# Cosine-similarity attention: the last pair in two pieces, six V buffers, and another order on every engine

## The chip, the cores and the metric

The kernel runs on one core of a Trainium2 chip. The metric is the device time of one launch in microseconds (us), lower is better.

## The reference

Q, K and V have the shape [8, 12, 512, 64] in float32 and tau is 0.1. For each of the 96 heads:

```python
Q_norm = Q / (np.linalg.norm(Q, axis=-1, keepdims=True) + 1e-10)
K_norm = K / (np.linalg.norm(K, axis=-1, keepdims=True) + 1e-10)
scores = np.einsum('bhqd,bhkd->bhqk', Q_norm, K_norm) / tau
weights = np.exp(scores - np.max(scores, axis=-1, keepdims=True))
weights = weights / (np.sum(weights, axis=-1, keepdims=True) + 1e-10)
return np.einsum('bhqk,bhkd->bhqd', weights, V).astype(np.float32)
```

A score is at most 1/tau = 10, so the kernel takes the exponential without the maximum.

## The kernel before

Two heads make a pair; there are 48 pairs, s = 0 to 47. A list of about 1800 operations, each named by a tuple, is built pair by pair. Which engine does an operation, and what it needs first, stands in the list; the order on each engine is written out by hand in `ORDER`, one row of operation numbers for SP, GpSimd ("pool"), VectorE ("dve"), TensorE ("pe") and ScalarE ("act"). Every engine works through its row in order and waits on semaphores where an operation's needs come from another engine.

The operations of pair s (w is 0 for Q, 1 for K; c counts the four chunks of 128 keys):

- `LD(s,w)` (L299, L296 for pair 0) and `LV(s)` (L302): loads of Q, K and V, 256 KB each, issued by SP. Q and K have 18 buffers, V has ten (`R_V`, the second number of `RINGS`): `LV(s)` needs `VC(s-10)`. `ST(s)` (L503) stores the pair's output; it stands in the same SP row, 12 places of pairs later, and waits for `NRM(s)`.
- `SQ(s,..)`: squares in bf16. From pair 4 on one GpSimd instruction over 1024 columns (L325); pairs 0 to 3 are cut by hand (`SQ_ON`, L319 on GpSimd, L317 on ScalarE). Pair 3 has one GpSimd instruction for Q and one for K.
- `SSQ(s,w)` (L342, TensorE) and `RED(s,w)` (L349 or L353, VectorE): sums of squares of each row.
- `LOG(g)` (L367) and `NEW(g,7)` (L370) on ScalarE for the groups g = 0 to 3 of one pair each: the inverse root as exp(-0.5 ln x). Later groups hold two or four pairs and take Newton steps `NEW(g,k)` on VectorE (L377 to L386).
- `SCL(s,w)` (L404; L246 for pair 0): the rows times the inverse root, in bf16, on VectorE or GpSimd. `TR(s,w)` (L410; L254, L256 for pair 0): four transposes on TensorE. `EVA(s)` (L417; L267 for pair 0): the copy from PSUM to SBUF on VectorE.
- `SCO(s,c)` (L446): the scores of chunk c for both heads, into one of two PSUM slots of two banks each. `EXP(s,c)` (L469): one exponential over 128 x 1024 on ScalarE. `SCO(s,c)` needs the exponential two chunks earlier. For pair 0 and c < 2 both are cut by head: `SCO(0,c,h)`, `EXP(0,c,h)`.
- `VC(s)` (L474): V in bf16 beside a column of ones, on GpSimd. `PV(s,h,i)` (L486): weights times V, with the row sums in column 64. `RCP(s,h)` (L497) and `NRM(s,h)` (L499): reciprocal of the sums and the scaled output on VectorE; `NRM(s)` needs `ST(s-8)`.

The last pair (function `last`) is cut into the entries of `PIECES` = (head, first, end) in blocks of 128 query rows: head 0 whole, head 1 in two halves. Its last exponential `EXP(47,3,k)` (L460), the products `PV(47,k,c)` (L514, one chunk c at a time), `RCP(47,k)` (L525), `NRM(47,k)` (L527) and the store `ST(47,k)` (L531) are made once per piece. Piece 2 accumulates in a spare bank. The store of piece 1 is issued by ScalarE, the others by SP:

```python
P.add(("ST", s, k), "act" if k == 1 else "sp", "ldh" if hi - lo == NT else "ldq", T0 + 100 if k == 1 else s + STORE_AT + k, [("NRM", s, k)],
```

At the start TensorE runs eight warm-up matmuls (L185) and between its first operations fills (L188, negative entries in `ORDER`: so many columns), whose results nobody reads.

Of the kernel before, what the change touches and what calls it, by code (L numbers as in the profile page):

```python
# [106 lines left out]
def bass_cosine_similarity_attention_kernel(  # L107
# [54 lines left out]
    group, first = [], []  # L162
# [122 lines left out]
    def pair(s):  # L285
# [6 lines left out]
        for w, x in ((0, Q), (1, K)):  # L292
            if s == 0:
                for h in range(2):
                    P.add(("LD", 0, w, h), "act" if w else "sp", "ldh", -1000 + h,  [],
                          lambda e, w=w, x=x, h=h: e.dma_start(out=qk[iq][:, w, h], in_=src(x, s)[:, h]), slot=f"head{w}_{h}")  # L296
                continue
            P.add(("LD", s, w), "sp", "ld1" if s == 1 else "ld", s, [*([("SCL", 0, w, 0), ("SCL", 0, w, 1), ("SQ", 0, w, 0), ("SQ", 0, w, 1)] if s == R_QK else [key("SCL", s - R_QK, w), *(squares(s - R_QK, w) if s >= R_QK else [])])],
                  lambda e, w=w, x=x: e.dma_start(out=qk[iq][:, w], in_=src(x, s)),  # L299
                  slot=f"first{s}_{w}" if s <= 3 else f"qk{iq}")  # L300
# [126 lines left out]
    def exps(s, c):  # L427
        if s < 0:
            return []
        if s == NP - 1 and c == NT - 1:  # L430
            return [("EXP", s, c, k) for k in range(3)]
# [109 lines left out]
PIECES = ((0, 0, 4), (1, 0, 2), (1, 2, 4))  # L541
GROUPS = [1, 1, 1, 1, 2, 2, 2, 2, 2, 2, 2, 2, 4]
SQ_ON = {1: ("act", ("act", "pool")), 2: ("act", "pool"), 3: ("pool", "pool")}
# [8 lines left out]
RINGS = 18, 10, 6, 3, 3, 3, 8, 3  # L552
# [17 lines left out]
def slack(s, most):  # L570
# [5 lines left out]
        "7 8 64 65 103 104 11 141 142 66 179 180 105 222 223 143 256 257 181 298 299 224 332 333 258 375 376 300 409 "  # L576
        "410 334 451 452 63 377 102 411 140 453 178 221 485 486 527 528 561 562 487 604 605 529 638 639 255 563 680 681 "
        "297 606 714 715 331 640 756 757 374 682 790 791 408 716 833 834 450 758 867 868 484 792 901 902 526 835 935 "
        "936 560 869 978 979 603 903 1012 1013 637 937 1046 1047 679 980 1080 1081 713 1014 1122 1123 755 1048 1156 "
        "1157 789 1082 1190 1191 832 1124 1224 1225 866 1158 1267 1268 900 1192 1301 1302 934 1226 1335 1336 977 1269 "  # L580
        "1369 1370 1011 1303 1412 1413 1045 1337 1446 1447 1079 1371 1480 1481 1121 1414 1514 1515 1155 1448 1556 1557 "
        "1189 1482 1590 1591 1223 1516 1624 1625 1266 1558 1658 1659 1300 1592 1700 1701 1334 1626 1734 1735 1368 1660 "
        "1768 1769 1411 1702 1445 1736 1479 1770 1513 1555 1589 1623 1657 1699 1733 1767 1797 1811 "
    ),
    "pool": (
        "2 0 1 4 14 27 22 35 69 107 50 144 145 89 182 225 127 165 259 208 301 231 335 378 273 284 307 242 454 412 437 "
        "350 395 471 361 318 488 530 426 460 564 607 641 502 536 683 513 717 579 547 759 590 793 836 655 689 870 624 "
        "666 904 742 731 765 700 938 981 808 819 776 876 1015 1049 910 1083 853 887 921 1125 1066 953 1159 987 964 1021 "
        "1108 998 1032 1193 1227 1270 1304 1097 1131 1210 1165 1338 1142 1372 1253 1321 1176 1199 1287 1415 1242 1310 "
        "1449 1483 1517 1344 1559 1432 1355 1466 1398 1500 1387 1421 1593 1455 1627 1576 1610 1661 1703 1737 1531 1565 "  # L590
        "1686 1644 1542 1599 1720 1771 1633 1754 1790 1675 1709 1743 1777 "
    ),
    "dve": (
        "5 13 15 26 28 19 24 21 32 37 71 73 34 109 78 111 76 80 116 114 147 149 118 152 154 183 156 185 226 228 55 186 "
        "56 187 188 61 189 62 190 94 191 95 193 192 194 195 197 100 262 101 199 260 302 304 229 263 138 264 139 265 233 "
        "266 132 267 133 268 338 269 270 176 271 170 379 171 305 275 177 213 336 214 219 381 220 339 340 309 341 342 "
        "455 343 253 344 345 346 348 247 415 248 413 347 352 382 254 289 457 384 416 290 417 386 295 418 296 419 489 "
        "420 323 421 491 423 324 329 422 330 424 458 428 531 366 533 367 492 372 493 565 494 373 495 462 496 608 497 "
        "400 567 401 499 498 406 500 407 642 504 534 610 442 568 443 569 448 570 449 571 684 572 538 573 476 575 574 "
        "644 577 477 611 718 581 482 576 483 613 686 518 645 519 646 760 647 615 648 524 649 525 650 552 720 652 651 "  # L600
        "553 653 837 794 558 657 796 559 595 762 687 721 596 722 871 723 691 724 601 725 839 726 602 728 629 873 727 "
        "630 729 635 905 636 733 763 907 671 797 798 672 799 677 800 801 678 802 767 804 803 939 806 705 941 706 840 "
        "711 805 712 810 982 908 842 747 984 748 753 754 844 874 1050 781 1018 782 787 788 878 1016 1084 1052 824 942 "
        "825 943 944 912 945 830 946 831 947 949 948 950 951 858 1086 859 864 865 985 955 1019 1160 898 899 892 1128 "
        "893 1126 989 1055 932 926 1162 927 933 1023 1053 1194 1196 969 1087 970 1088 975 1089 976 1090 1228 1091 1057 "
        "1092 1093 1094 1095 1129 1003 1230 1004 1009 1010 1099 1163 1037 1273 1038 1305 1133 1043 1044 1339 1071 1307 "
        "1072 1197 1271 1077 1078 1167 1373 1341 1113 1231 1114 1232 1233 1234 1119 1235 1120 1236 1238 1237 1201 1239 "
        "1240 1147 1375 1148 1276 1153 1154 1244 1274 1342 1181 1418 1182 1416 1450 1187 1278 1308 1188 1518 1215 1452 "
        "1216 1312 1484 1221 1222 1560 1486 1258 1376 1259 1377 1264 1378 1379 1265 1380 1346 1381 1382 1383 1385 1292 "
        "1520 1293 1384 1298 1299 1419 1389 1453 1326 1562 1332 1327 1333 1423 1489 1594 1360 1596 1361 1628 1366 1367 "  # L610
        "1457 1487 1630 1403 1521 1404 1522 1409 1523 1410 1524 1525 1662 1526 1491 1527 1528 1529 1443 1444 1563 1437 "
        "1664 1438 1738 1533 1477 1597 1478 1471 1706 1472 1631 1567 1704 1505 1740 1506 1601 1511 1772 1512 1774 1547 "
        "1665 1548 1666 1667 1668 1669 1670 1672 1671 1635 1673 1553 1554 1581 1582 1707 1677 1741 1587 1588 1711 1615 "
        "1616 1775 1621 1622 1649 1650 1745 1655 1656 1691 1692 1697 1698 1779 1725 1726 1731 1732 1759 1760 1765 1766 "
        "1802 1803 1795 1796 1809 1810 "
    ),
    "pe": (
        "6 -256 -256 -256 -192 23 20 -256 70 36 -128 42 72 33 38 108 39 43 110 46 79 77 48 146 81 148 117 83 115 51 85 "
        "57 58 52 53 87 59 54 153 119 155 184 121 60 227 123 125 90 91 92 93 157 96 97 98 159 99 128 261 161 196 198 "
        "163 134 135 136 200 137 303 129 202 130 232 204 230 131 172 206 173 174 175 337 234 166 167 168 169 236 272 "  # L620
        "238 274 209 240 210 211 212 380 276 215 216 217 218 278 306 308 280 243 249 244 282 250 251 252 310 245 246 "
        "414 312 349 314 351 285 286 316 287 288 456 353 383 291 355 292 293 385 357 294 319 320 321 359 322 490 325 "
        "387 326 327 328 389 362 363 364 365 391 427 425 393 368 532 369 429 370 459 371 431 461 396 433 397 398 399 "
        "435 566 402 463 403 404 405 465 438 439 440 441 467 501 503 469 609 444 445 505 446 447 535 507 537 472 473 "
        "509 474 475 643 511 478 479 539 480 481 541 578 580 543 514 515 516 545 517 685 582 612 520 521 584 614 522 "
        "523 586 548 549 550 551 588 719 616 554 555 556 557 618 591 795 592 620 654 656 622 593 594 761 658 690 597 "
        "598 660 599 600 688 662 838 625 626 664 627 628 872 692 631 632 694 633 634 667 668 696 730 732 698 669 670 "
        "906 734 673 674 675 676 736 764 766 738 701 702 703 740 704 940 768 707 708 709 770 710 807 772 809 743 744 "
        "774 745 746 749 811 841 983 813 750 751 752 815 843 777 778 817 779 783 780 784 845 1017 785 786 847 877 875 "
        "849 820 821 822 851 823 1051 826 879 911 909 881 827 828 829 883 854 855 856 885 857 1085 860 913 861 862 863 "  # L630
        "915 952 954 917 888 889 890 894 919 891 895 896 897 956 1127 986 958 988 928 929 960 930 922 923 931 962 924 "
        "925 1161 990 1020 1022 992 965 966 967 994 968 1195 971 996 972 973 974 1024 1054 1056 1026 999 1000 1028 1001 "
# [61 lines left out]
```

## Time and profile before

| | |
|---|---|
| runs | 191.13, 191.26, 191.09, 191.59 us; median 191.19 |
| profiled execution | 191.13 us; its span 189.0 us |
| granted TensorE clock | 1.0 |
| landing of a 256 KB load, from its issue | Q 4.3, K 5.4, V 5.2 us |
| landing of the last pair's stores | 128 KB 1.7, 64 KB 1.6 us |
| bytes moved | HBM read 37.75 MB, written 12.58 MB, 266 GB/s over the span |

A row of the profile names line, engine, operation and tile as out<-in; then come the count, the busy time with the mean in ns, and the idle time before it with what ended it. In the timeline a row has start, length, engine, line and operation; neighbours of one kind are merged ("x3"). Neighbouring instructions of one engine overlap in these records, so the pace is read from starts or ends, not from lengths. "q" behind an engine's name is its queue: it waits or issues.

### The profile page before, as it was taken

Reading aid. Unit: us, or ns where it says so; the run is one execution under the profiler, and the core shown is the slowest. Engines: PE = TensorE matmul, PEld = TensorE weight load, DVE = VectorE, ACT = ScalarE, POOL = GpSimd, SP = SyncE. Lnnn points to the kernel's source line nnn. Section 1 sums busy time; section 2 is a strip of 40 time slices with the busy share of each in tenths; the row PEclk is TensorE's granted clock in tenths of the full one; section 3 lists DMA queues with packets and bytes.
Section 4 is the critical chain, followed back from the end, with each engine's and each line's share of the span. In section 5 each row is a group of like instructions: output and inputs, shape, how many; then the busy total and the mean of one; then the engine's idle time right before and its main releaser. Section 6 shows DMA issues by size and latency. Waiting matters only on the chain.

```text
span 189.0 us, 6679 instructions
## 1 busy us (share of the span) xinstructions
PE 176.3 (93%) x2726; PEld 110.1 (58%) x2726; DVE 165.1 (87%) x530; ACT 182.1 (96%) x214; POOL 154.9 (82%) x145
## 2 busy tenths in 40 slices
PE   6998999999999999999999899999999999899992
PEld 2555666666565666566666566665666556555552
DVE  2788999999999999999999989998889987977543
ACT  4799999999999999999999999999999999999992
POOL 5599999999999999999999899999699898260000
PEclk9999999999999999999999999999999999999999
DMA  4999998899999898999899987996999944113133
GB/s 158 357 349 351 349 362 303 268 323 360 379 385 373 269 287 269 318 360 311 256 255 352 365 278 238 312 321 207 308 288 350 295 140 131 59 55 114 56 114 111
DMA packets 52445, 50.75 MB, mean 269 GB/s; under 512 B 3136, under 2 KB 52416, under 8 KB 52416
## 3 DMA queue, kind: packets, MB, share of 16 engines
q1 hardware_dynamic: 51984, 50.02, 82.0%
q8 instruction: 21, 0.34, 0.8%
q10 hardware_dynamic: 432, 0.33, 0.5%
q14 instruction: 8, 0.07, 0.1%
HBM read 37.75 MB, written 12.58 MB: 266 GB/s over the span
## 4 chain that ended last, share of the span: by engine, by line
ACT 94%; DMA 3%; SPq 1%; issue 1%; DVE 1%; PE 0%
ACT et L469 92%; DMA qk<-in_Q_dram 3%; SPq L299 0%; SPq L296 0%; ACT et L460 0%; DVE ob L527 0%; ACT sq L317 0%; ACT ys L367 0%; ACT nps L370 0%; PE ops L514 0%; DVE rd L525 0%
## 5 line engine op out<-in xcount | busy, mean ns | idle before, releaser
L469 ACT ACTIVATE et<-scps 128x1024 bf16<-128x1024 f32 (+1 forms) x193 | 175.8, 1249 | 0.0
L325 POOL TENSOR_TENSOR sq<-qk 128x1024 bf16<-128x1024 f32 x44 | 82.8, 1893 | 2.1 <-DMA qk<-in_K_dram 2.1
L446 PE MATMUL scps<-qt 64*128 64x512 bf16 x384 | 75.6, 386 | 7.5 <-ACT et L469 2.3
L486 PE MATMUL ops<-vb,et 128*128 128x65 bf16 x1504 | 74.5, 194 | 0.0
L486 PEld LDWEIGHTS ops<-vb,et 128*128 128x128 bf16 x1504 | 56.0, 98 | 27.9 <-issue 21.5
L404 POOL TENSOR_TENSOR qn<-qk,rk 128x512 bf16<-128x512 f32 x37 | 38.1, 1042 | 6.3 <-DVE rk L382 6.0
L499 DVE TENSOR_TENSOR ob<-ops,rd 128x256 f32<-128x256 f32 x94 | 39.3, 420 | 0.9
L404 DVE TENSOR_TENSOR qn<-qk,nps 128x512 bf16<-128x512 f32 x57 | 38.0, 678 | 0.5 <-ACT nps L370 0.5
L417 DVE COPY qt<-tps 128x1024 bf16<-128x1024 bf16 x47 | 32.3, 688 | 4.1 <-PE tps L410 3.4
L446 PEld LDWEIGHTS scps<-qt 64*128 64x128 bf16 x384 | 19.5, 93 | 26.3 <-ACT et L469 10.2
L410 PE MATMUL tps<-ident,qn 128*128 128x128 bf16 x376 | 33.0, 221 | 0.1
L474 POOL TENSOR_SCALAR vb<-vf 128x512 bf16<-128x512 f32 x48 | 29.3, 626 | 0.8 <-DMA vf<-in_V_dram 0.8
L353 DVE TENSOR_REDUCE nps<-sq 128x8 f32<-128x512 bf16 x44 | 29.7, 683 | 0.2 <-POOL sq L325 0.2
L410 PEld LDWEIGHTS tps<-ident,qn 128*128 128x128 bf16 x376 | 21.4, 98 | 11.9 <-issue 5.9
L497 DVE RECIPROCAL rd<-ops 128x4 f32<-128x4 f32 x94 | 16.6, 177 | 9.0 <-PE ops L486 5.8
L342 PE MATMUL ops<-sq,ident 128*128 128x64 bf16 x400 | 20.0, 193 | 0.3 <-ACT nps L240 0.3
L342 PEld LDWEIGHTS ops<-sq,ident 128*128 128x128 bf16 x400 | 14.9, 98 | 4.5 <-issue 2.9
L349 DVE TENSOR_REDUCE nps<-ops 128x8 f32<-128x64 f32 x44 | 9.3, 211 | 0.8 <-PE ops L342 0.7
L377 DVE TENSOR_TENSOR nps<-nps,ys 128x32 f32<-128x32 f32 (+1 forms) x30 | 6.2, 208 | 0.2
L378 DVE SCALAR_TENSOR_TENSOR nps<-nps,ys 128x32 f32<-128x32 f32 (+1 forms) x30 | 6.2, 207 | 0.2
L185 PE MATMUL ops<-warm_in,ident 128*128 128x512 bf16 x8 | 3.6, 631 | 1.4 <-POOL ident L175 1.4
L319 POOL TENSOR_TENSOR sq<-qk 128x512 bf16<-128x512 f32 (+1 forms) x4 | 3.7, 934 | 1.5 <-DMA qk<-in_K_dram 1.5
(50 smaller groups left out, 41.2 us busy)
## 6 DMA issues: line engine op xcount, KB each, us to landing
vf<-in_V_dram SPq DMA_DIRECT2D x48, 256.0 KB, 5.2
qk<-in_Q_dram SPq DMA_DIRECT2D x47, 256.0 KB, 4.3
qk<-in_K_dram SPq DMA_DIRECT2D x47, 256.0 KB, 5.4
out_dram<-ob SPq DMA_DIRECT2D x47, 256.0 KB, 3.7
qk<-in_Q_dram SPq DMA_DIRECT2D x2, 128.0 KB, 2.6
qk<-in_K_dram ACTq DMA_DIRECT2D x2, 128.0 KB, 2.8
out_dram<-ob SPq DMA_DIRECT2D x1, 128.0 KB, 1.7
out_dram<-ob ACTq DMA_DIRECT2D x1, 64.0 KB, 1.6
```

The lines of the kernel that those rows point to most:

```text
L325: lambda e: e.tensor_tensor(out=sqf, in0=data, in1=data, op=ALU.mult))
L342: last = e.matmul(out=o_ps[bank][:, 320:384], lhsT=ident[:, :], rhs=sq[iqs][:, 8 * w : 8 * w + 8, 8 * k : 8 * k + 8], start=(k == 0), stop ...
L353: lambda e, w=w, dst=dst: e.tensor_reduce(out=dst, in_=sq[iqs][:, 8 * w : 8 * w + 8, :], axis=AX.X, op=ALU.add))
L404: lambda e, w=w, r=r: e.tensor_tensor(out=qn[iqn][:, w].rearrange("p t h d -> p h t d"), in0=qk[iq][:, w].rearrange("p h (t d) -> p h t d" ...
L410: last = e.transpose(t_ps[:, w, t, :], qn[iqn][:, w, t].rearrange("p h d -> p (h d)"), ident[:, :])
L417: lambda e: e.tensor_copy(out=qt[iqt][:, :, :, :].rearrange("p w t x -> p (w t x)"), in_=t_ps[:, :, :, :].rearrange("p w t x -> p (w t x)")))
L446: last = e.matmul(out=sc_ps[:, 2 * b + h, :], lhsT=qt[iqt][64 * h : 64 * h + 64, 1, c, :], rhs=qt[iqt][64 * h : 64 * h + 64, 0, :, :], sta ...
L469: lambda e, c=c, b=b, hs=hs: e.activation(out=et[iet][:, c, hs[0] : hs[-1] + 1, :], in_=sc_ps[:, 2 * b + hs[0] : 2 * b + hs[-1] + 1, :], f ...
L474: lambda e: e.tensor_scalar(out=vb[:, iq, :, :, 0:DIM].rearrange("p c h d -> p h c d"), in0=vf[iv][:, :, :].rearrange("p h (c d) -> p h c ...
L486: last = e.matmul(out=o_ps[h][:, 65 * t : 65 * t + 65], lhsT=et[iet][:, c, h, 128 * t : 128 * t + 128], rhs=vb[:, iq, c, h, :], start=(c = ...
L497: lambda e, h=h, grid=grid: e.reciprocal(out=rd[io][:, h, :], in_=grid[:, :, DIM]))
L499: lambda e, h=h, grid=grid: e.tensor_tensor(out=ob[io][:, h], in0=grid[:, :, 0:DIM], in1=rd[io][:, h, :].unsqueeze(2).to_broadcast([128, N ...
```

## The change

Four places of the code and the five rows of `ORDER`:

```diff
-                  slot=f"first{s}_{w}" if s <= 3 else f"qk{iq}")
+                  slot=f"first{s}_{w}" if s <= 2 else f"qk{iq}")
...
-            return [("EXP", s, c, k) for k in range(3)]
+            return [("EXP", s, c, k) for k in range(len(PIECES))]
...
-PIECES = ((0, 0, 4), (1, 0, 2), (1, 2, 4))
+PIECES = ((0, 0, 4), (1, 0, 4))
...
-SQ_ON = {1: ("act", ("act", "pool")), 2: ("act", "pool"), 3: ("pool", "pool")}
+SQ_ON = {1: ("act", ("act", "pool")), 2: ("act", "pool")}
...
-RINGS = 18, 10, 6, 3, 3, 3, 8, 3
+RINGS = 18, 6, 6, 3, 3, 3, 8, 3
```

So the last pair has two pieces, one per head; pair 3's squares are one GpSimd instruction over Q and K, and its two loads count on one semaphore (`qk3`) in place of one each; V has six buffers, and `LV(s)` needs `VC(s-6)`. Nine operations fall away (the K half of pair 3's squares, and the third piece's exponential, four products, reciprocal, scaling and store).

The order, with numbers turned into names:

- SP: the same sequence, without the third piece's store at the end.
- ScalarE: the same sequence but for `LOG(1)`, which moves from behind `EXP(0,1,0)` to before it, and `LOG(3)`, which moves from before `EXP(1,1)` to behind it:

```diff
- SQ(2,0) EXP(0,1,0) LOG(1) NEW(1,7) EXP(0,0,0) EXP(0,0,1) EXP(0,1,1) LOG(2) EXP(0,2) NEW(2,7) EXP(0,3) EXP(1,0) LOG(3) EXP(1,1) NEW(3,7) EXP(1,2)
+ SQ(2,0) LOG(1) EXP(0,1,0) NEW(1,7) EXP(0,0,0) EXP(0,0,1) EXP(0,1,1) LOG(2) EXP(0,2) NEW(2,7) EXP(0,3) EXP(1,0) EXP(1,1) LOG(3) NEW(3,7) EXP(1,2)
```

- TensorE: two more fills of 256 columns before the first transposes, one more before `SSQ(1,1)`, which moves ahead of `SCO(0,1,0)`; `PV` of many pairs at other places between the scores. The beginning, and the end from the last scores on:

```diff
- warm 256 256 256 192 TR(0,1,0) TR(0,0,0) 256 SSQ(1,0) TR(0,1,1) 128 SCO(0,1,0) SSQ(1,1) TR(0,0,1) SCO(0,0,0) SSQ(2,0) SCO(0,0,1) SCO(0,1,1) SSQ(2,1) SCO(0,2) TR(1,1) TR(1,0) SCO(0,3) SSQ(3,0) SCO(1,0) SSQ(3,1) TR(2,1) SCO(1,1) TR(2,0)
+ warm 256 256 256 256 256 192 TR(0,1,0) TR(0,0,0) 256 SSQ(1,0) TR(0,1,1) 256 SSQ(1,1) 128 SCO(0,1,0) TR(0,0,1) SCO(0,0,0) SSQ(2,0) SCO(0,0,1) SCO(0,1,1) SSQ(2,1) SCO(0,2) TR(1,1) TR(1,0) SCO(0,3) SCO(1,0) SCO(1,1) SSQ(3,1) SSQ(3,0) TR(2,1) TR(2,0)
...
- SCO(47,3) PV(47,0,0) PV(47,1,0) PV(47,0,1) PV(47,1,1) PV(47,2,0) PV(47,1,2) PV(47,1,3) PV(47,0,2) PV(47,0,3) PV(47,2,1) PV(47,2,2) PV(47,2,3)
+ SCO(47,3) PV(46,0,2) PV(46,0,3) PV(47,1,0) PV(47,1,1) PV(47,1,2) PV(47,1,3) PV(47,0,0) PV(47,0,1) PV(47,0,2) PV(47,0,3)
```

- VectorE: `RED(1,0)`, `RED(1,1)` move ahead of `EVA(0,1,1)`; in some 150 places further on neighbours change places, mostly `RED`, `RCP` and `NRM` around `EVA`. At the end both pieces follow each other, head 1 first.
- GpSimd: the memset of `eps` moves behind the other three; `VC` of most pairs and some of `SQ` and `SCL` stand a few places earlier or later.

ScalarE's row ends with `EXP(47,3,1) EXP(47,3,0) ST(47,1)`, where it ended with `EXP(47,3,1) EXP(47,3,0) EXP(47,3,2) ST(47,1)`.

## The prediction

> **What bounds the kernel now.** I read the page first: shares, then the chain of waits, then the costliest groups.
>
> ```profile
> PE 176.3 (93%) x2726; PEld 110.1 (58%) x2726; DVE 165.1 (87%) x530; ACT 182.1 (96%) x214; POOL 154.9 (82%) x145
> L469 ACT ACTIVATE et<-scps 128x1024 bf16<-128x1024 f32 (+1 forms) x193 | 175.8, 1249 | 0.0
> ```
>
> ScalarE's exponentials (L469) are the chain and had no idle time before them. The mean of 1249 ns is no price, since neighbours overlap; the chain in order of time gives the pace:
>
> ```profile
> 15.06 169.56 ACT et L469 x185
> 184.63 0.78 ACT et L460 x2
> ```
>
> 169.56/185 = 0.917 us per exponential, without a gap. So the time has three parts: a head until about 15 us, a body that cannot get shorter while ScalarE does the same 185 exponentials, and a tail. A change in order can cost in the body and gain only at the two ends. Next I read ScalarE in the head:
>
> ```profile
> 8.36 0.58 ACT L469 ACTIVATE et<-scps 128x512 bf16<-128x512 f32 x1
> 8.84 0.30 ACT L367 ACTIVATE ys<-xs,eps 128x16 f32<-128x16 f32 x1
> 9.17 0.19 ACT L370 ACTIVATE nps<-ys 128x16 f32<-128x16 f32 x1
> 9.29 1.55 ACT L469 ACTIVATE et<-scps 128x512 bf16<-128x512 f32 x3
> 10.72 0.32 ACT L367 ACTIVATE ys<-xs,eps 128x16 f32<-128x16 f32 x1
> 10.92 1.03 ACT L469 ACTIVATE et<-scps 128x1024 bf16<-128x1024 f32 x1
> 11.82 0.21 ACT L370 ACTIVATE nps<-ys 128x16 f32<-128x16 f32 x1
> ```
>
> Every start follows the previous end: already here nothing but ScalarE's own order counts. A logarithm (L367) directly before its power (L370) takes 8.84 to 9.29 = 0.45 us; with an exponential between them the two cost 0.20 (10.72 to 10.92) plus 0.11 (11.82 to the next exponential at 11.93) = 0.31.
>
> **Head, TensorE's order.** The sums of pair 1's key squares, SSQ(1,1), move ahead of the first score, SCO(0,1,0). TensorE before:
>
> ```profile
> 7.52 0.22 PE L188 MATMUL scps<-warm_in,ident 128*128 128x128 bf16 x1
> 7.67 0.39 PE L446 MATMUL scps<-qt 64*128 64x512 bf16 x1
> 7.99 0.41 PE L342 MATMUL ops<-sq,ident 128*128 128x64 bf16 x8
> 8.23 0.39 PE L254 MATMUL tps<-ident,qn 128*128 128x128 bf16 x4
> 8.55 0.39 PE L446 MATMUL scps<-qt 64*128 64x512 bf16 x1
> ```
>
> SSQ(1,1) needs GpSimd's half square, whose row (start 7.16, 0.61 us) ends at 7.77; such sums start 0.05 to 0.09 after their square, so 7.84. From there by the rows' own steps: sums to the fill 0.24 (7.99 to 8.23), fill to score 0.15 (7.52 to 7.67), SCO(0,1,0) at 8.23; score to transposes 0.32, 8.55; to SCO(0,0,0) 0.32, 8.87; SSQ(2,0) 9.19; 0.34 later (8.87 to 9.21 before) SCO(0,0,1) at 9.53, where it stood at 9.21. Its result comes at 9.53 + 0.39 = 9.92, and the second exponential of the run at 9.29, which started at 9.77, starts at about 9.94: **+0.17 us**. The logarithm of group 1, now ahead of the first exponential, waits for its sum (7.84 + 0.41, then 0.23 on VectorE) and starts at about 8.53 in place of 8.84; its power no longer stands next to it, and the 0.14 that this saves is spent waiting for that score, so I count nothing. If the score came in time, it would be a gain of 0.1.
>
> **Head, ScalarE's order.** Group 3's logarithm moves behind EXP(1,1), directly before its power: 0.45 in place of 0.30 (13.73 to 13.93 and 14.84 to 14.94). **+0.15 us**. VectorE's SCL(3) waits for that power (0.48 us idle, then 15.10) and goes later by the same 0.3 as ScalarE, so the leads further on stay.
>
> **Head, the rest, at nothing.** Two more 256-column fills before the first transposes cost at most 2 x 0.21 us (the half-rate fills start 4.83, 5.04, 5.25), and the eps memset moved back gives up to 0.10. The transposes at 5.89 go back by 0.2 at most; the copies they feed end at 7.09, while the next reader on TensorE's path is now at 8.23, so about 0.9 us covers it. Without that cover it would be 0.2. The third new fill stands where TensorE waits for 7.77 anyway. Pair 3's squares as one GpSimd instruction cost 1.89 (the L325 row at 13.15) in place of 2.04 for both: 0.15 earlier on an engine that next waits 0.29 for a load. Sharing one semaphore among pair 3's two loads costs nothing, as that square needs both.
>
> The Trainium skill's "TensorE: Matmul & The Clock Gate" (Part 1, What's actually happening) lets the full rate begin after about 3.4 us of steady work; here 256-column fills still start 0.21 apart at 5.25, 3.8 us after the first matmul at 1.44. By the rule the two extra fills would cost 0.22 us together, by the row 0.43; both are covered.
>
> **Body, six V buffers.** LV(s) now waits for VC(s-6). I set each V load's issue beside the conversion six earlier, GpSimd's places taken from the new order: 16 of 42 come too early, by 0.1 to 4.5 us. The worst:
>
> ```profile
> 63.56 1.50 SPq L302 DMA_DIRECT2D vf<-in_V_dram  x1
> 65.10 0.47 SPq L299 DMA_DIRECT2D qk<-in_Q_dram  x1
> ```
>
> ```profile
> 67.95 1.21 POOL L474 TENSOR_SCALAR vb<-vf 128x512 bf16<-128x512 f32 x2
> ```
>
> LV(21) stands until 68; behind it in SP's queue are pair 24's Q and K loads (65.10 to about 68.5) and the stores. Pair 24's squares start at 74.2 and its scaling at 92.5: the delay goes into that distance. From pair 12 on every load was issued 16 us or more before its scaling (least at pair 12: 34.0 to 50.0), of which landing takes about 5, and stores waiting for L499 already hold SP for 46.4 us in all. I count nothing; the other end is rival 2.
>
> **Body, reordering.** EVA (L417) to the pair's first exponential leaves as little as 0.59 us (pair 16) where ScalarE has no gap. Adding up VectorE's durations ahead of each EVA in both orders: EVA(8) has 0.41 more before it and had 0.90 of lead, leaving 0.49, 0.10 short; EVA(16) has 0.41 more, but VectorE idled 0.33 before it, so 0.08 short. All others keep 0.59. Both losses: **+0.2 us**. From both sides: 0 if the least lead seen isn't the least needed, 1.0 if none of the roughly 0.4 us shifts at the tight pairs (8, 16 and one further) is absorbed. I take 0.2, near the low end, because most pairs keep their lead.
>
> **Tail.** VectorE before:
>
> ```profile
> 185.23 0.17 DVE L525 RECIPROCAL rd<-ops 128x2 f32<-128x2 f32 x1 [0.71 <-PE ops L514]
> 185.44 0.29 DVE L527 TENSOR_TENSOR ob<-ops,rd 128x128 f32<-128x128 f32 x1
> 185.78 0.18 DVE L525 RECIPROCAL rd<-ops 128x4 f32<-128x4 f32 x1
> 186.00 0.42 DVE L527 TENSOR_TENSOR ob<-ops,rd 128x256 f32<-128x256 f32 x1
> 186.53 0.29 DVE L527 TENSOR_TENSOR ob<-tps,rd 128x128 f32<-128x128 f32 x1
> ```
>
> Three pieces end at 186.82. After: the last whole exponential ends at 184.62 (two from 182.45, 2.17 us); two of 512 columns at 0.49 each (three took 1.55 in the head) end at 185.11 and 185.60 (before 185.67). Head 1: product 185.16 to 185.47 (0.31 in the chain), reciprocal to 185.67, scaling 185.71 to 186.13. Head 0: product ends 185.96, but VectorE is free only at 186.05; reciprocal to 186.23, scaling 186.27 to 186.69. That is 0.13 earlier. Its store is 128 KB in place of 64: 1.7 us to landing against 1.6. **-0.03 us**. That ScalarE issues the second head's store is no news: before, too, it issues piece 1; nothing is queued behind it there, and its issue (0.35) is over before SP's. SP loses one issue (0.42), the last. Bounds: -0.4 (all of the third piece's 0.40 behind 186.42) and +0.1.
>
> The Trainium skill's "DMA: Bandwidth & Descriptors" (Anatomy of one DMA) speaks against joining pieces at the end: a fixed part and then bytes/436e9, so 64 KB more would be 0.15 us as an estimate. The rows say 0.1; the tail would be +0.02 by the rule.
>
> **Sum.** The profiled execution took 191.13 us (span 189.0). 191.13 + 0.17 + 0.15 + 0.2 - 0.03 = 191.62; the median of the runs is 0.06 above that execution: **191.7 us, +0.27%**. About 0.2% (0.38 us) is what a measurement here can tell from no change.
>
> **Rivals.**
> 1. The body keeps its pace and only the head slips: 191.19 + 0.29 = 191.5, within 0.2%. For it: no gap in 185 exponentials before, and the same work. Against: the tight leads of pairs 8 and 16.
> 2. SP's queue becomes the bound: the V waits push loads so late that GpSimd stands still and the scalings behind it come late. Delays of 3.4 to 4.5 us at LV(21), LV(32) and LV(34), less what the distances cover; if 1 us of it reaches ScalarE, 191.7 + 1.0 = 192.7. For it: 16 waits, and GpSimd's five waits for K loads (2.1 us) show that it can be starved. Against: some 10 us between landing and scaling.
> 3. Faster: the third piece was dear. If the score lands in time (head +0.0), the logarithm gains 0.1 and the tail all of 0.4, 191.19 - 0.5 = 190.7. It decides if head 1's product ends 0.1 us or more earlier than I have it, so that VectorE is free when head 0's arrives. Against: the two scalings of 0.42 in a row.
>
> **Chances.** Forecast 0.48 (191.4 to 192.0; a quarter of it within 0.2%), rival 1 0.22, rival 2 0.18, rival 3 0.12. Slower by over 0.2%: 0.36 + 0.02 + 0.18 = 0.56; within: 0.12 + 0.18 + 0.03 = 0.33; faster: 0.02 + 0.09 = 0.11. Range 191.0 to 192.6: leaves out rival 3 and the upper half of rival 2.
>
> **What would show it.** SCO(0,0,1) at 9.5 and the second 512 exponential after 9.29 at about 9.94; L370 directly behind L367 at about 15.2; the first of the long run of exponentials 0.3 late; SP's waits for L474 up from 3.3 to over 15 us; idle time before L469 near 8 and 16 pairs in; last L527 near 187.2 with the whole shift in. It is wrong if the long run starts no later than 15.1, or if ScalarE's gaps add to over 0.5 us.

## The result, and the profile after

Over 53 runs of the changed kernel and 79 of the kernel before, the medians are 191.7 and 191.2 us: **ratio 1.0024, 95% interval 1.0015 to 1.0034**. The change costs about 0.45 us. The medians are of all runs; the ratios leave out the few executions that were over 1.5% slower than the fastest of their kernel. The profiled execution of the changed kernel took 192.02 us (span 189.9).

The costliest group on the page of the changed kernel:

```profile
L469 ACT ACTIVATE et<-scps 128x1024 bf16<-128x1024 f32 (+1 forms) x193 | 175.8, 1234 | 0.0
```

The same 193 exponentials, the same 175.8 us, and again no idle time before them. This says that the body did not change and the loss lies at the ends. The chain of waits of the changed kernel in order of time (start, duration, what), from the landing of pair 1's K load on:

```profile
2.16 5.43 DMA qk<-in_K_dram
7.59 0.07 issue
7.66 0.62 POOL sq L319
8.28 0.14 issue
8.42 0.39 PE ops L342 x8
8.81 0.06 PE scps L188
8.87 0.32 PE scps L446
9.18 0.33 PE tps L254 x4
9.51 0.32 PE scps L446
9.83 0.34 PE ops L342 x8
10.17 0.33 PE scps L446
10.51 0.02 issue
10.53 1.09 ACT et L469 x2
...
15.58 0.20 ACT ys L367
15.77 0.02 issue
15.80 0.19 ACT nps L370
15.99 169.59 ACT et L469 x185
```

The same view of the kernel before, for its first exponentials:

```profile
2.67 5.14 DMA qk<-in_Q_dram
7.80 0.02 issue
7.83 0.63 ACT sq L317
8.46 0.48 ACT et L469
8.94 0.20 ACT ys L367
9.14 0.02 issue
9.17 0.19 ACT nps L370
9.36 1.49 ACT et L469 x3
```

The reader is to see three things. Before, the first exponentials hung on the landing of pair 2's Q load (7.80) and then on ScalarE's own row: its square of that load (L317), EXP(0,1,0), group 1's logarithm and power, EXP(0,0,0), and EXP(0,0,1), which started at 9.77. The head now hangs on pair 1's key square (L319), then on its sums (L342), and only then come pair 0's scores (L446): that is the new TensorE order. Group 3's logarithm and power (L367, L370) stand next to each other and both lie on the chain. And the body is 169.59 us for 185 exponentials, against 169.56 before.

The head starts from loads, and these do not land at the same time in every execution. So I read each profile by stages between fixed events (times of single instructions and landings in the trace, us; each difference is one subtraction):

| stage | before | after | change |
|---|---|---|---|
| pair 1's K load landed | 7.09 | 7.59 | +0.50 |
| from there to the start of EXP(0,0,1) | 2.68 | 2.94 | +0.26 |
| end of EXP(1,0) to end of EXP(1,2) | 2.13 | 2.27 | +0.14 |
| pair 2's Q load landed to end of EXP(1,2) (the whole head behind the loads) | 8.21 | 8.62 | +0.41 |
| end of EXP(1,2) to end of the last whole exponential (body) | 168.62 | 168.66 | +0.04 |
| from there to VectorE's last instruction | 2.19 | 2.07 | -0.12 |
| from there to the end of the span | 2.21 | 2.28 | +0.07 |

The row of 2.68 and 2.94 is the distance from a fixed event, not one path: before, that exponential waited for pair 2's Q load, 0.71 us behind pair 1's K load, and not for pair 1's.

0.51 (pair 2's Q load landed at 7.80 before and at 8.31 after) + 0.41 + 0.04 - 0.12 + 0.07 = 0.91, and the spans differ by 189.93 - 189.03 = 0.90. The later landing is half of what separates the two profiles, and 0.40 is left for the kernel itself, close to the 0.45 of the medians. Whether the landing belongs to the change is the first question for the experiments.

### The profile page after: what moved, and what is told of

Its sections match the earlier page's. It is cut to its first block, busy times and chain, and to the rows that moved or that the text cites. A ratio compares the mean times of both kernels' runs of the same rounds, so it can differ in the third digit from the quotient of the medians.

```text
span 189.9 us, 6675 instructions
## 1 busy us (share of the span) xinstructions
PE 176.6 (93%) x2729; PEld 110.2 (58%) x2729; DVE 164.9 (87%) x528; ACT 182.3 (96%) x213; POOL 154.9 (82%) x144
## 4 chain that ended last, share of the span: by engine, by line
ACT 92%; DMA 3%; PE 1%; issue 1%; SPq 1%; DVE 1%; POOL 0%
ACT et L469 91%; DMA qk<-in_K_dram 3%; PE scps L446 1%; DVE ob L527 0%; SPq L296 0%; PE ops L342 0%; POOL sq L319 0%; ACT et L460 0%; SPq L299 0%; ACT ys L367 0%; ACT nps L370 0%; PE tps L254 0%; PE ops L514 0%; DVE rd L525 0%; PE scps L188 0%
## 5 line engine op out<-in xcount | busy, mean ns | idle before, releaser
L469 ACT ACTIVATE et<-scps 128x1024 bf16<-128x1024 f32 (+1 forms) x193 | 175.8, 1234 | 0.0
L325 POOL TENSOR_TENSOR sq<-qk 128x1024 bf16<-128x1024 f32 x45 | 84.6, 1893 | 2.4 <-DMA qk<-in_K_dram 1.4
L446 PE MATMUL scps<-qt 64*128 64x512 bf16 x384 | 75.6, 386 | 7.7 <-ACT et L469 2.1
L486 PE MATMUL ops<-vb,et 128*128 128x65 bf16 x1504 | 75.7, 194 | 0.0
L446 PEld LDWEIGHTS scps<-qt 64*128 64x128 bf16 x384 | 19.4, 93 | 27.2 <-ACT et L469 13.0
L342 PE MATMUL ops<-sq,ident 128*128 128x64 bf16 x400 | 19.7, 193 | 0.9 <-ACT nps L240 0.6
L342 PEld LDWEIGHTS ops<-sq,ident 128*128 128x128 bf16 x400 | 14.9, 98 | 3.5 <-issue 1.6
L382 DVE SCALAR_TENSOR_TENSOR nps<-nps,ys 128x16 f32<-128x16 f32 (+1 forms) x22 | 3.9, 183 | 0.1
```

The costliest lines, as they stand in the source:

```text
L325: lambda e: e.tensor_tensor(out=sqf, in0=data, in1=data, op=ALU.mult))
L342: last = e.matmul(out=o_ps[bank][:, 320:384], lhsT=ident[:, :], rhs=sq[iqs][:, 8 * w : 8 * w + 8, 8 * k : 8 * k + 8], start=(k == 0), stop ...
L446: last = e.matmul(out=sc_ps[:, 2 * b + h, :], lhsT=qt[iqt][64 * h : 64 * h + 64, 1, c, :], rhs=qt[iqt][64 * h : 64 * h + 64, 0, :, :], sta ...
L469: lambda e, c=c, b=b, hs=hs: e.activation(out=et[iet][:, c, hs[0] : hs[-1] + 1, :], in_=sc_ps[:, 2 * b + hs[0] : 2 * b + hs[-1] + 1, :], f ...
L486: last = e.matmul(out=o_ps[h][:, 65 * t : 65 * t + 65], lhsT=et[iet][:, c, h, 128 * t : 128 * t + 128], rhs=vb[:, iq, c, h, :], start=(c = ...
```

## The experiments

All 12 kernels compute the whole reference. In the diffs below the places in the order are given by operation names. The theory from the stage table: the whole loss is in the head, 0.26 us of it on pair 1's path (TensorE's order) and 0.14 on group 3's path (ScalarE's order); buffers, body order and tail come to nothing together. The rivals: the loads land later because of the change, and SP's waits for V buffers cost something.

**First set: the buffers alone, and the head's parts taken back one at a time.** (Ratios to the kernel before on the same chip, 34 runs of it, median 191.05.)

`b_v6` is the kernel before with six V buffers:

```diff
-RINGS = 18, 10, 6, 3, 3, 3, 8, 3
+RINGS = 18, 6, 6, 3, 3, 3, 8, 3
```

> The kernel before with six V buffers in place of ten and nothing else (its own orders). Theory (the whole loss is in the head, the body loses nothing): 191.2 us, within 0.1% of before; SP's wait for L474 rises from 3.3 us to 15 us or more, and the last whole exponential still ends 169.6 us after the first of the long run (185 at 0.917 us). Rival (the V waits push loads late until ScalarE has gaps): 191.5 us or more, idle time before L469 above 0.2 us.

Measured: 192.64 us, **1.0086 [1.0058, 1.0113]**, 11 runs, which is the rival. It is discussed with the second set, where it is answered.

`a_pair1` is the changed kernel with pair 1's path as before:

```diff
 pe
-TR(0,1,1) 256 SSQ(1,1) 128 SCO(0,1,0) TR(0,0,1)
+TR(0,1,1) 128 SCO(0,1,0) SSQ(1,1) TR(0,0,1)
 dve
-RED(1,0) RED(1,1) EVA(0,1,1)
+EVA(0,1,1) RED(1,0) RED(1,1)
 act
-LOG(1) EXP(0,1,0)
+EXP(0,1,0) LOG(1)
```

> The changed kernel with the path of pair 1's key squares put back: SSQ(1,1) behind SCO(0,1,0) without the extra fill, EVA(0,1,1) ahead of RED(1,0), LOG(1) behind EXP(0,1,0). Theory: 0.17 to 0.25 us comes back, 191.45 us; SCO(0,0,1) starts within 2.2 us of the landing of pair 1's K load (2.5 us in the changed kernel's profile, 2.1 in the one before). Rival (the first loads simply land later in the changed kernel, 7.59 against 7.09 us for pair 1's K): the time stays at 191.7 and the load still lands near 7.6.

Measured: 191.36 us, 1.0022 [1.0007, 1.0037], 12 runs. TensorE's timeline of this kernel (start, busy us of the group, what):

```profile
8.59 0.39 PE L446 MATMUL scps<-qt 64*128 64x512 bf16 x1
8.90 0.41 PE L342 MATMUL ops<-sq,ident 128*128 128x64 bf16 x8
9.15 0.39 PE L254 MATMUL tps<-ident,qn 128*128 128x128 bf16 x4
```

Pair 1's K load landed at 8.00 in this execution, later than in the changed kernel's profile, and yet EXP(0,0,1) started 2.72 after it, where the changed kernel took 2.94 and the kernel before 2.68. The score (8.59) runs while GpSimd is still at the square (8.00 + 0.07 + 0.62, so until about 8.69); behind the sums (8.90) the transposes follow at once (9.15), with no fill and no score between. The chain of waits comes from pair 2's Q load again (landed at 8.76) and runs over ScalarE, with EXP(0,0,1) 1.96 behind that landing; in the kernel before it is 1.97. So in the profiles 0.22 us of the loss goes when pair 1's path is put back. Three rows were put back together; that it is TensorE's order that counts is read from the changed kernel's chain, which holds no VectorE row and no logarithm between 7.59 and 10.53. The time does not show it: 1.0022 is the ratio of the whole change (1.0024), and the interval also holds the 1.0012 that was to be expected. The run also speaks against the change as a cause of the late loads: with part of it undone they landed later still.

`a_grp3` is the changed kernel with group 3's path as before:

```diff
-SQ_ON = {1: ("act", ("act", "pool")), 2: ("act", "pool")}
+SQ_ON = {1: ("act", ("act", "pool")), 2: ("act", "pool"), 3: ("pool", "pool")}
...
 pool: SQ(3,1) behind SQ(3,0), and the slot of pair 3's loads as before
 pe
-SCO(0,3) SCO(1,0) SCO(1,1) SSQ(3,1) SSQ(3,0) TR(2,1) TR(2,0)
+SCO(0,3) SSQ(3,0) SCO(1,0) SSQ(3,1) TR(2,1) SCO(1,1) TR(2,0)
 dve: RED(3,0) ahead of RED(3,1)
 act
-EXP(1,1) LOG(3)
+LOG(3) EXP(1,1)
```

> The changed kernel with group 3's path put back: pair 3's squares in two halves, SSQ(3,0) ahead of SCO(1,0), RED(3,0) first, LOG(3) ahead of EXP(1,1). Theory: the logarithm and its power apart cost 0.30 in place of 0.45, so 0.15 us comes back: 191.55 us, and from the end of EXP(1,0) to the end of EXP(1,2) it takes 2.13 us in place of 2.28. Rival (nothing is won since EXP(1,1) or EXP(1,2) waits for its scores): 191.7 us, and a gap before L469 there.

Measured: 191.33 us, 1.0022 [1.0005, 1.0039], 12 runs. The stage from EXP(1,0) to EXP(1,2) fell to 2.15, which is what was expected; the pair 1 path stayed at 2.94. The time does not show it, for 0.14 us is below what 12 runs can tell, and this profile lost 0.52 us in the body (169.18 against 168.66). Its GpSimd and its ScalarE, from their timelines, with the idle time before an instruction and what ended it in brackets:

```profile
101.03 1.89 POOL L325 TENSOR_TENSOR sq<-qk 128x1024 bf16<-128x1024 f32 x1 [1.15 <-DMA qk<-in_K_dram]
103.63 1.89 POOL L325 TENSOR_TENSOR sq<-qk 128x1024 bf16<-128x1024 f32 x1 [0.71 <-DMA qk<-in_K_dram]
```

```profile
108.42 17.62 ACT L469 ACTIVATE et<-scps 128x1024 bf16<-128x1024 f32 x19 [0.34 <-PE scps L446]
```

Two K loads came late. The chain of waits leads from the second of these squares over VectorE's row and TensorE to a gap of 0.34 us before the last exponential of pair 26. The body of this kernel is the changed kernel's, so the changed order has places where it can be starved in single executions; in the changed kernel's own profile it was not.

`a_head` takes back both paths, and the two extra fills and the place of `eps`: the head of the kernel before, the body and tail of the changed one.

```diff
 (a_pair1 and a_grp3 together)
 pe
-warm 256 256 256 256 256 192
+warm 256 256 256 192
 pool
-one eye vone eps
+eps one eye vone
```

> The changed kernel with the whole head order of before (both paths put back, the two extra fills out, eps first), but its own body, six V buffers and two last pieces. Theory: 191.1 us, that is before less 0.1 for the tail; the long run of exponentials starts about 6.4 us after the landing of pair 2's Q load, as before. Rival (part of the loss lies in body or tail): 191.3 us or more.

Measured: 190.98 us, **1.0005 [0.9990, 1.0020]**, 12 runs: as the kernel before. So the loss is in the head, as far as the interval tells; `b_head` below asks the same from the other side. In its profile the body took 168.64 and the tail 2.07 + 2.27, as in the changed kernel.

**Second set: are the buffers free, and why?** (Before: 191.12, 29 runs.) Six buffers alone had cost 0.86%, more than the whole change, which has six buffers too. Three kernels ask what the changed kernel does about it.

`a_v10` is the changed kernel with ten V buffers (`RINGS = 18, 10, ...`):

> The changed kernel with ten V buffers and nothing else. Theory (six buffers still cost something in executions whose loads are late, as GpSimd then waits for a K load near 100 us): 0.05 to 0.2 us faster than the changed kernel, 191.5 us, and GpSimd no longer idle before pair 34's squares. Rival (the body is free of it, all of the loss is head): 191.7 us.

Measured: 191.54 us, 1.0031 [1.0012, 1.0051], 12 runs. No faster than with six, and the body of its profile takes the same 168.65: in the changed kernel the six buffers cost nothing that these runs can tell.

`b_v6_pool` is the kernel before with six buffers and GpSimd's whole order from the changed kernel (pair 3's squares still in halves), everyone else's order as before:

> The kernel before with six V buffers and with GpSimd's order taken from the changed kernel (pair 3's squares still in halves); the other engines in before's order. The six buffers alone cost 0.86%. Theory (GpSimd's earlier V conversions are what makes six buffers nearly free): half or more of that comes back, 191.9 us or less, and SP's wait for L474 falls from 23.8 us to about 16, as in the changed kernel. Rival (the conversions' place does not matter, the other engines' orders do): 192.5 us or more.

Measured: 196.78 us, **1.0310 [1.0268, 1.0352]**, 6 runs, against what I expected. GpSimd's new order moves squares and scalings too, and these no longer fit VectorE's and TensorE's old orders. From this kernel's waits (engine, line, whom it waits for: us in total, times, longest):

```profile
POOL qn L404 <- DVE rk L382: 8.5, 5, 3.5
```

GpSimd's scalings stand up to 3.5 us for VectorE's norms, and behind them stand the next squares. The kernel shows that GpSimd's order can't be carried over alone; on the V conversions it says nothing.

`b_v6_vc`, run with the third set, is the clean version: the kernel before with six buffers, where only the conversions VC stand at their places in the changed kernel among GpSimd's squares and scalings. 25 of 48 move; around pair 24, for example:

```diff
-SQ(23,0) VC(18) SCL(18,1) SCL(19,1) VC(17) SQ(24,0) SQ(25,0) SCL(20,1) VC(20) VC(19) SCL(22,1) SQ(26,0) SQ(27,0) SCL(23,1) SQ(28,0) VC(21) VC(22) VC(23) SQ(29,0) VC(27)
+SQ(23,0) SCL(18,1) VC(17) SCL(19,1) VC(18) VC(19) SQ(24,0) SQ(25,0) SCL(20,1) SCL(22,1) VC(20) SQ(26,0) VC(21) VC(22) SQ(27,0) SCL(23,1) SQ(28,0) SQ(29,0) VC(25) VC(23)
```

> The kernel before with six V buffers and only the V conversions at the changed kernel's places between GpSimd's squares and scalings, whose own order stays as before. Six buffers alone cost 0.86%; with GpSimd's whole order 3.1%. Theory (late conversions hold SP, late loads starve GpSimd): half or more of the 0.86% comes back, 191.9 us or less, and the gaps before EXP(23,2) and EXP(27,2) (0.6 us each) are gone. Rival (the places must fit all engines' orders): 192.5 us or more, with gaps elsewhere.

Measured: 191.04 us, **0.9993 [0.9974, 1.0011]**, 12 runs against 35 of before. All of the 0.86% comes back, and the body of its profile (168.62) has no gap. How six buffers cost it in `b_v6` can be followed engine by engine: SP, GpSimd, TensorE and ScalarE on its timelines.

```profile
68.60 0.37 SPq L302 DMA_DIRECT2D vf<-in_V_dram  x1
...
78.24 0.47 SPq L503 DMA_DIRECT2D out_dram<-ob  x1
81.68 0.37 SPq L302 DMA_DIRECT2D vf<-in_V_dram  x1
...
85.41 0.56 SPq L299 DMA_DIRECT2D qk<-in_K_dram  x1
```

```profile
74.95 1.89 POOL L325 TENSOR_TENSOR sq<-qk 128x1024 bf16<-128x1024 f32 x1 [0.75 <-DMA qk<-in_K_dram]
77.58 1.89 POOL L325 TENSOR_TENSOR sq<-qk 128x1024 bf16<-128x1024 f32 x1 [0.74 <-DMA qk<-in_K_dram]
...
80.44 1.21 POOL L474 TENSOR_SCALAR vb<-vf 128x512 bf16<-128x512 f32 x2
...
91.78 1.89 POOL L325 TENSOR_TENSOR sq<-qk 128x1024 bf16<-128x1024 f32 x1 [0.81 <-DMA qk<-in_K_dram]
...
94.22 1.04 POOL L404 TENSOR_TENSOR qn<-qk,rk 128x512 bf16<-128x512 f32 x1
```

```profile
95.33 0.40 PE L410 MATMUL tps<-ident,qn 128*128 128x128 bf16 x4 [0.88 <-POOL qn L404]
95.65 0.39 PE L446 MATMUL scps<-qt 64*128 64x512 bf16 x2
```

```profile
96.09 6.52 ACT L469 ACTIVATE et<-scps 128x1024 bf16<-128x1024 f32 x7 [0.58 <-PE scps L446]
```

It begins with the longest wait. SP stands from 63.31 to 68.60 in front of pair 21's V load (L302), whose buffer GpSimd has not yet converted; pair 24's K load behind it is issued at 69.53, in the kernel before at 65.62. GpSimd waits 0.75 us for it and 0.74 us for pair 25's (74.95, 77.58), and its next two conversions stand behind these squares (80.44, in the kernel before 79.01). So SP stands again, from 78.71 to 81.68, for the second of them. Loads and store queue up behind that wait; the last line of SP is pair 29's K load, at 85.41, in the kernel before at 82.70. GpSimd's square of that pair (91.78) waits 0.81 us for it. The scaling behind the square (94.22) comes late, the transposes of its result wait 0.88, and in TensorE's row the next score stands behind these transposes, so that ScalarE waits 0.58 us for it, before EXP(23,2). Such a gap stands twice in the body (the other is 0.59, before EXP(27,2)), and the body takes 170.01 in place of 168.62.

The two totals that matter, of `b_v6` and then of `b_v6_vc`, from their waits:

```profile
SPq L302 <- POOL vb L474: 23.8, 13, 5.3
...
POOL sq L325 <- DMA qk<-in_K_dram: 4.4, 7, 0.8
```

```profile
SPq L302 <- POOL vb L474: 19.6, 15, 3.2
...
POOL sq L325 <- DMA qk<-in_K_dram: 1.7, 4, 0.7
```

With the conversions moved SP still waits 19.6 us; but the longest wait is 3.2 us in place of 5.3, and GpSimd waits for loads no more than before (2.1 us). In the changed kernel SP waits 15.7 us in 15 times, at most 3.3. The sums are not far apart, so it is not the sum of the waits that costs. Nor is it the length of each wait by itself: the one up to 81.68 is 2.97 us, shorter than the 3.2 and 3.3 that cost nothing in the other two kernels. As far as these profiles show, a wait costs when the loads behind it land after GpSimd is ready for them.

`b_tail` is the kernel before with two pieces at the end:

```diff
-PIECES = ((0, 0, 4), (1, 0, 2), (1, 2, 4))
+PIECES = ((0, 0, 4), (1, 0, 4))
...
-            return [("EXP", s, c, k) for k in range(3)]
+            return [("EXP", s, c, k) for k in range(len(PIECES))]
...
 pe
-SCO(47,3) PV(47,0,0) PV(47,1,0) PV(47,0,1) PV(47,1,1) PV(47,2,0) PV(47,1,2) PV(47,1,3) PV(47,0,2) PV(47,0,3) PV(47,2,1) PV(47,2,2) PV(47,2,3)
+SCO(47,3) PV(47,0,0) PV(47,0,1) PV(47,0,2) PV(47,1,0) PV(47,1,1) PV(47,1,2) PV(47,1,3) PV(47,0,3)
```

> The kernel before with the last pair in two pieces and nothing else (head 0's first three chunks, then head 1, then head 0's last chunk on TensorE). Theory: from the end of the last whole exponential to the last scaling 2.07 us in place of 2.19, and the last store 0.1 longer to land: 0.0 to 0.1 us faster, 191.1 us. Rival (joining the pieces lengthens the end): 191.3 us or more.

Measured: 191.34 us, 1.0006 [0.9987, 1.0024], 12 runs. VectorE ended 2.07 after the last whole exponential, the span 2.30 later: -0.12 and +0.09 against the kernel before. The two-piece tail is worth nothing that can be measured.

`a_head_v10` is `a_head` with ten buffers:

> The changed kernel with the head of before and ten V buffers: what is left of the change is two last pieces and the order of the body. Theory: before less 0.1, 191.0 us. Rival (the body's order is worse by itself): 191.3 us or more.

Measured: 191.41 us, 1.0008 [0.9990, 1.0026], 12 runs. Its loads landed at 7.26 and 7.96, nearly as in the profile of before, and the head behind them took 8.21, exactly as before. The loss is not seen with the head taken back, though this interval alone would also hold it.

**Third set: the head alone, put into the kernel before.** (Before: 191.12, 35 runs.) `b_head` is the kernel before with the changed kernel's whole head and nothing else: TensorE's order up to TR(2,0), LOG(1) and LOG(3), VectorE's first sums, pair 3's squares whole, the fills, `eps`.

> The kernel before with the changed kernel's whole head and nothing else: all of TensorE's order up to pair 2's transposes, LOG(1) and LOG(3), the order of the sums of pairs 1 and 3, pair 3's squares in one, the fills. Ten V buffers and three last pieces stay. Theory (the loss is the head): 0.41 us slower, 191.5 to 191.6 us; from the landing of pair 2's Q load to the end of EXP(1,2) 8.6 us in place of 8.2. Rival (a part of the loss needs the changed body): 0.2 us or less.

Measured: 191.58 us, **1.0023 [1.0005, 1.0042]**, 12 runs: the ratio of the whole change. Its stages are the changed kernel's: 2.94, 2.27, 8.60; body 168.65.

`b_adj` moves one instruction, LOG(3) behind EXP(1,1):

```diff
-EXP(1,0) LOG(3) EXP(1,1) NEW(3,7) EXP(1,2)
+EXP(1,0) EXP(1,1) LOG(3) NEW(3,7) EXP(1,2)
```

> The kernel before with LOG(3) moved behind EXP(1,1), directly before its power, and nothing else. Theory: 0.15 us; from the end of EXP(1,0) to the end of EXP(1,2) 2.28 us in place of 2.13, and all that follows shifts with it. Rival (the shift is taken up again within the next pairs): the stage is longer, but the last whole exponential ends as early as before.

Measured: 190.99 us, 0.9999 [0.9980, 1.0017], 12 runs. ScalarE's timeline of this kernel:

```profile
14.52 0.35 ACT L367 ACTIVATE ys<-xs,eps 128x16 f32<-128x16 f32 x1
14.90 0.19 ACT L370 ACTIVATE nps<-ys 128x16 f32<-128x16 f32 x1
15.03 4.66 ACT L469 ACTIVATE et<-scps 128x1024 bf16<-128x1024 f32 x5
```

The stage is 2.27 as in the changed kernel, against 2.13 before, by this one move: 0.14 us. The time can't confirm it, since 0.14 us is 0.07% and the interval is 0.19% wide on each side.

`b_ssq` moves SSQ(1,1) alone ahead of the fill and of SCO(0,1,0):

```diff
-TR(0,1,1) 128 SCO(0,1,0) SSQ(1,1) TR(0,0,1)
+TR(0,1,1) SSQ(1,1) 128 SCO(0,1,0) TR(0,0,1)
```

> The kernel before with SSQ(1,1) moved ahead of the fill and of SCO(0,1,0), and nothing else. Theory: from the landing of pair 1's K load to the start of EXP(0,0,1) 2.9 us in place of 2.68, 0.2 us slower. Rival (it is LOG(1) and the order of the sums on VectorE that cost, not TensorE's order): 2.7 us, no slower.

Measured: 191.05 us, 1.0000 [0.9980, 1.0021], 12 runs. The time is inconclusive, since 0.2 us is 0.1%. In the profiled execution pair 1's K load landed at 6.37, early enough for SSQ(1,1) to start at 7.44, directly behind the transposes ahead of it. TensorE's and ScalarE's timelines:

```profile
7.44 0.44 PE L342 MATMUL ops<-sq,ident 128*128 128x64 bf16 x8
```

```profile
8.30 0.60 ACT L469 ACTIVATE et<-scps 128x512 bf16<-128x512 f32 x1 [0.53 <-PE scps L446]
```

SSQ(1,1) itself waited for nothing, but the first score stood behind it (the fill between them starts at 7.71, 0.27 us after the sums), and ScalarE waited 0.53 us for that score; EXP(0,0,1) started 2.61 behind pair 2's Q load, where the kernel before takes 1.97. TensorE's granted clock was also lower in this execution, 0.92 between 5 and 8 us, and pair 0's transposes came later (6.05 against 5.89), so the 2.61 is not the move's alone.

So the size of the TensorE term rests on `a_pair1` and on the kernels that carry one order or the other whole, not on this run. Over the 14 profiles the chain to EXP(0,0,1) is one of three. In the nine kernels with the old TensorE order it comes from pair 2's Q load and runs over ScalarE: 1.96 to 1.97 us behind that landing in six, 2.11 to 2.16 in three (`a_head`, `b_tail`, `b_v6_pool`), where LOG(1) waits for its sum. In the changed kernel, `a_grp3` and `b_head` it runs over TensorE as shown, 2.94 behind pair 1's K load and 2.20 to 2.22 behind pair 2's Q load (in the last two TensorE's earlier work ended within 0.07 us of the start of the sums, so these were nearly as late without the load). In `a_v10`, which has the new head too, pair 1's K load landed at 6.00, and the chain does not come from any load of pair 1 or 2:

```profile
1.41 3.59 PE ops L185 x8
5.00 1.23 PE scps L188 x6
```

From these warm-up matmuls and fills on TensorE works, without a wait that the trace shows, up to the score of EXP(0,0,1), which starts at 9.74; in `a_head`, with the old head and pair 2's Q load landing at 7.17 against 7.08, it starts at 9.28. So where loads land early, everything that the new order puts ahead of the scores counts. How the 0.46 us divides between the fills and the sums was not tried.

**The landing of the first loads.** Over the 14 profiles pair 1's K load landed between 6.00 and 8.00 us: 6.00 (`a_v10`) and 7.59 (after) share the whole head, 6.51 (`a_head`) and 7.26 (`a_head_v10`) too, and the latest is `a_pair1`. The 0.50 by which the changed kernel's profile was behind therefore needs no cause in the change: it lies within what executions of one head differ by.

No version was found that is clearly faster than the kernel before: `a_head`, `a_head_v10`, `b_tail` and `b_v6_vc` are all within their intervals of it.

## Why the prediction was right

Forecast 191.7, measured 191.7; slower, as the likeliest case had it. The exact hit is luck. The terms were 0.49 us in sum and the profiles show 0.40, with two errors of opposite sign: the head was taken 0.09 too cheap, the body 0.16 too dear.

1. **TensorE's order, +0.17 predicted, +0.26 measured.** The mechanism was right (pair 1's sums ahead of a score that was ready, so that ScalarE waits for TensorE) and so were the steps behind it: from the first score on 0.32 to 0.34 each. The term was mis-sized at its beginning: the sums started 0.14 us behind their square (8.28 to 8.42), where I took 0.07. SCO(0,0,1) at 10.11 and the exponential at 10.53, less the 0.50 of the landing, are each 0.1 later than the 9.5 and 9.94 that I named as signs.
2. **ScalarE's order, +0.15 predicted, +0.14 measured** (2.27 against 2.13; alone in `b_adj`).
3. **Rest of the head at nothing:** right for the changed kernel's profile, where the two terms leave 0.41 - 0.26 - 0.14 = 0.01. As a rule it was wrong: the cover of about 0.9 us that I gave the new fills was TensorE's wait for pair 1's load, and in `a_v10`, where that load landed early, TensorE did not wait.
4. **V buffers at nothing: right for the change, but for a reason I had not given.** I argued that the distances between loads and their use would cover SP's waits (predicted over 15 us, measured 15.7). `b_v6` shows that these distances do not cover them in the old order: 0.86%. By `b_v6_vc` it is enough that the V conversions stand where the six buffers need them (the changed kernel with the old places was not run); I had read their new places as input to a sum, not as the cover itself. The distance that I measured, load to scaling (16 us or more), was also the wrong one: the first to read a load is the square, which for pair 24 starts at 74.2, 8.6 us behind the issue of its K load (65.62), and it is the squares that stood still in `b_v6`.
5. **Body order, +0.2 predicted, +0.04 measured: the failed step.** I took the least lead seen without a gap, 0.59 us at pair 16, as the least that is needed, and found pairs 8 and 16 short of it by 0.10 and 0.08. In the changed kernel these two had leads of 0.66 and 0.68, and others ran with 0.55 (pair 1) and 0.56 (pair 12) and still no gap. So 0.59 was no threshold, and adding up the durations ahead of an instruction overstated how late it comes: EVA(8) lost 0.24 of lead where I had 0.41, and EVA(16) gained 0.09. Why was not followed.
6. **Tail, -0.03 predicted, -0.05 measured:** VectorE 0.12 earlier (0.13 predicted), the end of the span 0.07 later behind it (0.1 predicted for the larger store). VectorE's timeline of the changed kernel:

```profile
186.68 0.42 DVE L527 TENSOR_TENSOR ob<-ops,rd 128x256 f32<-128x256 f32 x1
187.02 0.17 DVE L525 RECIPROCAL rd<-ops 128x4 f32<-128x4 f32 x1
187.23 0.42 DVE L527 TENSOR_TENSOR ob<-ops,rd 128x256 f32<-128x256 f32 x1
```

The two scalings of 0.42 follow each other with only a reciprocal between, as laid out; that is what eats the gain of the dropped piece. The estimate of 0.15 us for 64 KB more, from the Trainium skill's "DMA: Bandwidth & Descriptors" (Anatomy of one DMA), is about twice what the end of the span shows, 0.07. That section's fit is for transfers issued by GpSimd, and these stores are issued by SP and ScalarE.

Of the signs that the prediction named, SP's waits (15.7 us) and the power directly behind its logarithm (15.45 and 15.80) came as it said. The last scaling started at 187.23 and ended at 187.65; the 187.2 was meant for its end (186.69 and the shift of 0.52), so it came 0.44 later than that, within the 0.51 of the late landing, and the likeness of 187.23 is chance. Further, the long run of exponentials starts 0.93 later (15.06 to 15.99), of which 0.51 is the landing and 0.41 the head; the idle time before L469 near pairs 8 and 16 did not come, which is point 5.

Of the rivals, the first (only the head slips) is the nearest to what happened in kind: the body kept its pace. Its price of 0.29 was too low, since the head costs 0.41. The second (SP's queue) is what the six buffers do without the new order: its price of 1 us is close to the 1.4 that the body of `b_v6` lost, and single executions of the changed body can still lose something of the kind, 0.52 in `a_grp3`, though whether SP's waits were the cause there was not followed. The third (faster by the tail) fell with `b_tail`.

## What to carry to other kernels

Where one engine sets the pace from end to end, cut the profile into stages between landings and fixed instructions before comparing two executions: the start of the loads moves by more than the change. In this kernel a smaller ring of buffers was paid for not by the sum of its waits but by the loads queued behind them, where these landed after their reader was ready, and the order of the instructions that free the buffers decided that; change and test ring size and order together. Do not count work as covered by a wait for a load from one execution alone: when the load lands early, the cover is gone. Ahead of a bound engine, put work that waits for a late load behind work that is ready, and keep two short dependent instructions apart when something can run between them.

## What the runs showed of the hardware

- The landing of the first loads is not a constant of the kernel: pair 1's K load, issued at about 2 us, landed between 6.00 and 8.00 us over 14 profiles, and in the changed kernel's profile it took 5.43 us (2.16 to 7.59).
- TensorE's sums SSQ(1,1) started 0.14 to 0.15 us behind GpSimd's square in the three profiles where the new order waits for it (after, `a_grp3`, `b_head`), where others of their kind took 0.05 to 0.09; what makes the difference was not tried.
- The moment from which TensorE's fills run at double pace is not a constant of the kernel either: fills of 256 columns still started 0.21 us apart up to 5.65 us in the changed kernel's profile and up to 5.87 in those of `a_v10` and `b_head`, 4.2 and 4.5 us behind the first matmul (1.41), while in `b_adj` they started 0.10 to 0.11 apart from 4.58 on, 3.1 us behind it (1.44).
